# The fourth block of a recurrent layer's gates as three rounded products, gathered from the parts of the other blocks

## The chip, the cores and the metric

The kernel runs on one core of a Trainium2 chip. The metric is the device time of one execution in microseconds (us); before the change it is 1038.47 us, the median of 3 runs (1038.31 to 1038.69). Engines are named as in the profile: PE multiplies matrices, PEld is its weight load, DVE, ACT and POOL work on elements, and SP issues most transfers (its rows are marked SPq).

## The reference, cut to what matters

A two-layer decoder trunk takes one step on 1024 prompt tokens and 8 sequences of 4 sample tokens, 1056 columns in all. The first layer is a gated linear recurrence of width 1536, the second another recurrence that the change does not touch. In the first layer every token passes a projection, a short convolution that gives `xf`, and two gates whose weights are block diagonal, 16 blocks of 96 by 96:

```python
xh = xf.reshape(Bsz, T, N_BLK, BLK_W)                       # 16 blocks of 96
r  = sigmoid(einsum('btni,nij->btnj', xh, w_r).reshape(Bsz, T, W) + b_r)
ig = sigmoid(einsum('btni,nij->btnj', xh, w_i).reshape(Bsz, T, W) + b_i)
log_a = -LRU_C * softplus(-lam) * r
a = exp(log_a)
bterm = sqrt(-expm1(2.0 * log_a)) * (ig * xf)
_, h = associative_scan(_lru_combine, (a, bterm), axis=1)   # h[t] = a[t] h[t-1] + bterm[t]
```

## The kernel before, in words

Columns are cut into three chunks of 352 (`CH`). The layer's 1536 rows lie in 12 tiles of 128 rows; three tiles make a group `g` (0 to 3), and four blocks of 96 rows share a group. Tile `j` (0 to 2) holds block `j` and, in its rows 32j to 32j+31, a third of the fourth block. So blocks 0 to 2 are multiplied where they lie, and the fourth must first be gathered from three tiles.

Nearly all matrix work is done as three rounded products (`mm3`, lines 287 to 291): each operand is split into a rounded part and the rounded remainder, and high by high, high by low and low by high are summed in one accumulator. A convolution's result `t` is split that way into two slices of the tile `X` (`xpart`, lines 412 to 415; the split is on lines 596 and 597). The function `lru` (line 629) then computes the gates of a group, chunk by chunk, for both weights (`i` is 0 and 1): three rounded products for each of the three tiles (lines 653 and 654), a tanh into the tile `R`, and for the fourth block one product in full precision on 96 rows (line 659), a tanh into the tile `td`, and three transfers that put the thirds back into `R` (line 665). The fourth block's input comes from the tile `ST`: while a chunk is convolved, one transfer for each tile copies 32 rows of `t` there (line 594). Its weights `gs` are loaded as they are (line 639). After the gates follow exponentials, a square root, products and a scan on DVE, ACT and POOL.

The order of all this is not that of the code. Every operation is recorded with a rough cost, and with keys for what it reads and writes (`Flow`, line 61); a planner orders the operations of each engine by list scheduling, backward passes and a random search over the first part, and the program then has that order on every engine, each of which runs its own list from the top. A key names a tile or a piece of it: a write waits for the last reads of that key. Transfers from SP run through that one list too. Before the gates, each chunk of the input is normalised: squares are summed (ACT squares, line 491, DVE adds, line 493), PE sums over rows (line 326) and spreads the inverse root over the rows (line 545), and DVE scales eight tiles (line 550) and subtracts their rounded parts (line 374) to get what PE multiplies. With chunk 0 the scaling comes after the product instead. ACT also takes chunk 1's and 2's squares along rows of a transposed copy (line 532).

Of the kernel before, what the change touches and what calls it, by code (L numbers as in the profile page):

```python
# [14 lines left out]
F32 = mybir.dt.float32  # L15
F32R = mybir.dt.float32r
# [3 lines left out]
ALU = mybir.AluOpType  # L20
# [30 lines left out]
CH = 352  # L51
# [3 lines left out]
ML = WL // 128  # L55
# [202 lines left out]
def tile_trunk(ctx: ExitStack, tc: tile.TileContext, xT, xN, prm, hc, w0, wg, wo0, w1, wo1, s_in,  # L258
# [11 lines left out]
    def C(name, dt=F32):  # L270
        return work.tile([128, TOK], dt, tag="C", bufs=9, name=name)
# [12 lines left out]
    def chunk(c):  # L284
        return slice(c * CH, (c + 1) * CH)
# [59 lines left out]
    with ExitStack() as l0:  # L345
# [3 lines left out]
        def fixed(name, shape, dt=F32, pool=None):  # L349
            return (pool or pl).tile(shape, dt, tag=name, name=name)  # L350
# [7 lines left out]
        def dma(dst, src, r=(), w=(), prio=5, kb=180, q=Q, chain=None):  # L358
            fl.add("SP" if q is Q else "ACT", 0.45, lambda: q.dma_start(dst, src), r, w, prio, kb * (1.0 if r or fl.exact else 0.75),
                   line=chain)  # L360
# [8 lines left out]
        def pool(n, emit, r, w, prio=5):  # L369
            fl.add("POOL", 0.13 + 0.0022 * n if fl.exact else 0.1 + 0.00245 * n, emit, r, w, prio)  # L370
# [29 lines left out]
        hst = fixed("hst", [128, ML, 9])  # L400
# [153 lines left out]
        def conv(g, head=False):  # L554

            items = []
            for j in range(3):
                m = 3 * g + j
                mine = {}

                def evac(c, ps, pk, by=None, j=j, m=m, mine=mine):
                    n = CH if c < 2 else 1024 - 2 * CH
                    if c == 0:
                        mine[0] = next(xbs)
                        pool(3, lambda xb=mine[0][0]: G.memset(xb[:, :3], 0.0), (), (mine[0][1],), 2)
                    elif head:
                        mine[c] = next(xbs)
                        pool(3, lambda xb=mine[c][0]: G.tensor_copy(xb[:, :3], tails[:, 4 * j:4 * j + 3]), (("tail", j),), (mine[c][1],), 0)
                    xb, xk = mine[c]
                    t, tk = next(ts)  # L570
                    if by:
                        dve(n, lambda: V.tensor_tensor(xb[:, 3:3 + n], ps[:, :n], by[0], op=ALU.mult), (pk, by[1]), (xk,), 0)
                        pool(3, lambda: G.tensor_copy(tails[:, 4 * j:4 * j + 3], xb[:, n:n + 3]), (xk,), (("tail", j),), 1)
                    else:
                        act(n, lambda: S.copy(xb[:, 3:3 + n], ps[:, :n]), (pk,), (xk,), 0)
                    if c < 2 and not by:
                        nx, nk = mine[c + 1] = (tails[:, 4 * j:], ("tail", j)) if head else next(xbs)
                        act(3, lambda: S.copy(nx[:, :3], ps[:, CH - 3:CH]), (pk,), (nk,), 0)
                    parts = [(xb[:, :3 + n], t[:, :n], lambda ap, i: ap[:, i:i + n], n)]
                    if c == 2:  # L580
                        xs = xb[:, 323:379].rearrange("p (b j) -> p b j", j=7)
                        pool(24, lambda: G.tensor_copy(xs[:, :, :3], cs[:, m]), (("hct",),), (xk,), 1)
                        act(32, lambda: S.copy(xs[:, :, 3:], ps[:, n:CH].rearrange("p (b j) -> p b j", j=4)), (pk,), (xk,), 0)
                        pool(3, lambda: G.tensor_copy(cst[:, m, 0, :], xb[:, 320:323]), (xk,), (("cst", m),), 4)
                        pool(24, lambda: G.tensor_copy(cst[:, m, 1:, :], xs[:, :, 4:7]), (xk,), (("cst", m, 1),), 4)
                        parts.append((xs, t[:, n:].rearrange("p (b j) -> p b j", j=4), lambda ap, i: ap[:, :, i:i + 4], 32))
                    for src, dst, sh, u in parts:
                        act(u, lambda src=src, dst=dst, sh=sh: S.activation(dst, sh(src, 3), AF.Identity, bias=pc("cb", m),  # L588
                                                                         scale=pc("cw", 36 + m)), (xk, ("P",)), (tk,), 1, 0.1)
                        for k in range(3):  # L590
                            dve(u, lambda src=src, dst=dst, sh=sh, k=k: V.scalar_tensor_tensor(  # L591
                                dst, sh(src, k), pc("cw", 12 * k + m), dst, op0=ALU.mult, op1=ALU.add), (xk, tk), (tk,), 1, True)
# [36 lines left out]
        def lru(g):  # L629
            for i, n in ((0, 4), (4, 2)):  # L630
# [5 lines left out]
                act(u, lambda raw=raw, hi=hi, u=u: S.copy(hi, raw[:, :u]), (rk,), (("gh", i),), 2)  # L636
                pool(u, lambda raw=raw, hi=hi, lo=lo, u=u: G.tensor_tensor(lo, raw[:, :u], hi.bitcast(F32), op=ALU.subtract),
                     (rk, ("gh", i)), (("gl", i),), 2)
            dma(gs.rearrange("p a b -> p (a b)"), wg[g][:96, 768:], (), (("gs",),), 2, 74, chain=SPQ)
            prev = [(0.0, None)] * 3  # L640
            for c in range(NCH):
                s = c % 2
# [1 line left out]
                ab = a_rows[s].rearrange("p (j n) -> p j n", j=3)  # L644
                ta, ti = R[:, 0], R[:, 1]
                tak, tik = ([("R", s, i, j) for j in range(3)] for i in range(2))
                for i, hb in ((0, hbr), (1, hbi)):
                    for j in range(3):
                        m = 3 * g + j
                        ps, pk = next(hg)  # L650
                        (a, ak), (b, bk) = xpart(j, 0, c), xpart(j, 1, c)
                        u = 3 * i + j
                        fl.add("PE", 0.48, lambda ps=ps, a=a, b=b, u=u: mm3(ps[:, :CH], (gh[:, u, :], gl[:, u, :]), a, b, True, True),
                               (ak, bk, ("gh", u // 4 * 4), ("gl", u // 4 * 4)), (pk,), 0)
                        act(CH, lambda ps=ps, R=R, i=i, j=j, hb=hb, m=m: S.activation(R[:, i, j], ps[:, :CH], AF.Tanh, bias=hb[:, m:m + 1],  # L655
                                                                           scale=0.5), (pk, ("sm",)), (("R", s, i, j),), 2, 0.05)
                    ps, pk = next(hg)

                    fl.add("PE", 0.62, lambda ps=ps, i=i, c=c: T.matmul(ps[:96, :CH], gs[:, i, :], ST[:96, chunk(c)], start=True, stop=True),  # L659
                           (("gs",), *(("ST", j, c) for j in range(3))), (pk,), 0)  # L660
                    act(CH, lambda ps=ps, i=i: S.activation(td[:, i], ps[:96, :CH], AF.Tanh, bias=hbd[:96, 4 * i + g:4 * i + g + 1],
                                                            scale=0.5), (pk, ("sm",)), (("td", i),), 2, 0.05)
# [19 lines left out]
                for j in range(3):  # L682
# [13 lines left out]
                           (("a", s, j), tik[j], *((ppk,) if ppk else ())), (hk,), 3, both=True)  # L696
                    prev[j] = h[:, CH - 1:CH], hk
                    if c == 2:
                        pool(1, lambda h=h, m=m: G.tensor_copy(hst[:, m, 0:1], h[:, 319:320]), (hk,), (("hst", m),), 4)
                        pool(8, lambda h=h, m=m: G.tensor_copy(hst[:, m, 1:], h[:, 320:].rearrange("p (b j) -> p b j", j=4)[:, :, 3]),  # L700
                             (hk,), (("hst", m, 1),), 4)
                    if late:
                        continue
                    sg, sk = sgs[g][j, c]
# [356 lines left out]
        dma(h_out, hst.rearrange("p m b -> p (m b)"), [("hst", m) for m in range(ML)] + [("hst", m, 1) for m in range(ML)], (), 8)  # L1061
        out_last(x1b)
        for i, c in ((0, 0), (0, 1), (1, 0), (1, 1), (0, 2), (1, 2)):
            first1(i, c)
# [923 lines left out]
```

## Time and profile before

| what | value |
|---|---|
| runs of the kernel, median (lowest to highest) | 1038.47 us (1038.31 to 1038.69) |
| span of the profiled execution | 1036.8 us |
| what lies around the span, against the median | 1.7 us |
| PE busy | 1027.5 us (99%), 9789 matrix instructions |
| DVE, ACT, POOL busy | 794.4, 591.1, 500.0 us (77, 57, 48%) |
| share of PE in the chain that ended last | 95% |
| DVE busy from 60 to 160 us, and from 360 to 420 us | 94.20 of 100, 55.52 of 60 us |
| the full-precision product of the fourth block (L659) | 48 instructions, 458 ns each |

A row of the timeline has the start and the duration in us, the engine, the line of the code, the operation, the output and the inputs by the program's names, the shapes, how many were merged, and in brackets how long the engine stood idle before and what ended that. A product in full precision shows as two matrix instructions. A matrix instruction's duration runs over its successor's start, so what one costs PE is read from the distance between starts. The granted clock is 0.998 of full speed over the span.

### The profile page before, as it was taken

The page shows a single profiled execution, that of the slowest core. Times are in us where ns is not written, and L with a number is a line of the kernel's source. Part 1 is how long each engine was busy: PE and PEld are TensorE (multiplying, and loading weights), DVE is VectorE, ACT ScalarE, POOL GpSimd, SP SyncE. Part 2 cuts the span into 40 slices and gives each one's busy share as a digit, 9 for nine tenths or more (in the row PEclk, how much of TensorE's full clock was granted, in tenths as well). Part 3 has the DMA queues.
Part 4 walks back from the last instruction along what each step waited for, and adds up shares of the span by engine and source line. Part 5 has one row for each costly group of instructions (what it writes and reads, how often), then busy time and mean ns, then how long its engine had stood idle before and what let it go on. Part 6 is the DMA issues. An engine that isn't in the chain of part 4 may idle for free.

```text
span 1036.8 us, 25400 instructions
## 1 busy us (share of the span) xinstructions
PE 1027.5 (99%) x9789; PEld 998.9 (96%) x9789; DVE 794.4 (77%) x1548; ACT 591.1 (57%) x1346; POOL 500.0 (48%) x577
## 2 busy tenths in 40 slices
PE   9999999999999999999999999999999999999997
PEld 9999999999999999999999999999999999999986
DVE  5898996888897599355498986887869696985437
ACT  6678657867675775234355464737464555752324
POOL 2334553354443365644617565554645555541544
PEclk9999999999999999999999999999999999999999
DMA  8611112223751585444654241423233242658204
GB/s 280 196 37 49 53 50 75 61 62 112 231 166 55 174 275 184 145 154 153 196 173 145 76 158 41 152 71 126 83 107 122 84 143 86 211 159 252 87 1 168
DMA packets 92810, 133.56 MB, mean 129 GB/s; under 512 B 11728, under 2 KB 70096, under 8 KB 92688
## 3 DMA queue, kind: packets, MB, share of 16 engines
q1 hardware_dynamic: 84048, 117.14, 35.5%
q10 hardware_dynamic: 8640, 14.79, 4.5%
q8 instruction: 77, 1.26, 0.5%
q14 instruction: 45, 0.37, 0.1%
HBM read 88.81 MB, written 38.20 MB: 123 GB/s over the span
## 4 chain that ended last, share of the span: by engine, by line
PE 95%; DVE 2%; DMA 1%; ACT 1%; POOL 0%; issue 0%; ACTq 0%; POOLq 0%; DVEq 0%
PE mm L289 27%; PE mm L291 26%; PE mm L290 26%; PE hg L1202 2%; PE hg L659 1%; PE hg L289 1%; PE hg L291 1%; PE hg L290 1%; PE hg L1417 1%; PE hg L1419 1%; PE hg L1365 1%; PE mm L1365 1%; PE hg L1461 1%; DMA a<-in_w_dram 1%; DMA sg<-in_xT_dram 1%; PE hg L1287 0%
## 5 line engine op out<-in xcount | busy, mean ns | idle before, releaser
L289 PE MATMUL mm<-xh,whi 128*128 128x352 f32 (+1 forms) x1127 | 351.8, 312 | 0.0
L291 PE MATMUL mm<-xh,wlo 128*128 128x352 f32 (+1 forms) x1127 | 347.7, 309 | 0.0
L290 PE MATMUL mm<-xl,whi 128*128 128x352 f32 (+1 forms) x1127 | 347.2, 308 | 0.0
L374 POOL TENSOR_TENSOR wlo<-wraw,whi 128x256 fp32r<-128x256 f32 (+3 forms) x180 | 196.7, 1111 | 194.3 <-ACT whi L433 108.5
L290 PEld LDWEIGHTS mm<-xl,whi 128*128 128x128 f32 x1127 | 212.2, 188 | 1.7
L289 PEld LDWEIGHTS mm<-xh,whi 128*128 128x128 f32 x1127 | 211.9, 188 | 1.9
L291 PEld LDWEIGHTS mm<-xh,wlo 128*128 128x128 f32 x1127 | 211.8, 188 | 0.0
L591 DVE SCALAR_TENSOR_TENSOR k<-xb,prm_sb,k 128x352 f32<-128x352 f32 (+2 forms) x144 | 87.6, 616 | 12.7 <-ACT k L588 7.6
L289 PE MATMUL mm<-t,whi 128*128 128x264 f32 (+1 forms) x330 | 96.8, 293 | 0.0
L290 PE MATMUL mm<-t,whi 128*128 128x264 f32 (+1 forms) x330 | 94.4, 286 | 0.0
L291 PE MATMUL mm<-t,wlo 128*128 128x264 f32 (+1 forms) x330 | 94.4, 286 | 0.0
L374 POOL TENSOR_TENSOR wlo<-R,whi 128x256 fp32r<-128x256 f32 x78 | 67.2, 885 | 44.8 <-ACT whi L1582 33.1
L674 POOL TENSOR_TENSOR k<-X 128x352 f32<-128x352 f32 x36 | 43.4, 1216 | 58.1 <-DVE R L675 41.1
L1659 DVE TENSOR_TENSOR k<-mm,k 128x264 f32<-128x264 f32 x118 | 49.6, 425 | 24.1 <-PE mm L291 22.8
L289 PEld LDWEIGHTS mm<-t,whi 128*128 128x128 f32 x330 | 62.1, 188 | 1.3 <-DVE sg L1659 0.3
L291 PEld LDWEIGHTS mm<-t,wlo 128*128 128x128 f32 x330 | 62.2, 188 | 0.0
L290 PEld LDWEIGHTS mm<-t,whi 128*128 128x128 f32 x330 | 62.1, 188 | 0.0
L433 ACT CAST whi<-wraw 128x512 fp32r<-128x512 f32 (+2 forms) x79 | 44.1, 571 | 25.4 <-PE mm L290 9.3
L289 PE MATMUL mm<-yh,whi 128*128 128x352 f32 x153 | 50.0, 327 | 0.0
L291 PE MATMUL mm<-yh,wlo 128*128 128x352 f32 x153 | 49.4, 323 | 0.0
L290 PE MATMUL mm<-yl,whi 128*128 128x352 f32 x153 | 49.4, 323 | 0.0
L655 ACT ACTIVATE R<-hg,smalls 128x352 f32<-128x352 f32 x72 | 37.5, 553 | 17.9 <-DVE R L695 10.7
(482 smaller groups left out, 2502.7 us busy)
## 6 DMA issues: line engine op xcount, KB each, us to landing
wraw<-in_w_dram SPq DMA_DIRECT2D x54, 256.0 KB, 3.0
wraw<-in_w_dram ACTq DMA_DIRECT2D x34, 256.0 KB, 3.5
wraw<-in_wo_dram SPq DMA_DIRECT2D x34, 192.0 KB, 2.5
R<-in_w_dram ACTq DMA_DIRECT2D x19, 256.0 KB, 2.6
si<-in_s_in_dram SPq DMA_DIRECT2D x8, 512.0 KB, 5.9
vt<-sg SPq DMA_DIRECT2D x8, 512.0 KB, 3.1
sg<-vt SPq DMA_DIRECT2D x32, 128.0 KB, 3.0
kt<-kt SPq DMA_DIRECT2D x8, 512.0 KB, 2.6
```

The source lines that it names most:

```text
L289: T.matmul(out, wh, xh, start=first, stop=False, skip_group_check=more)
L290: T.matmul(out, wh, xl, start=False, stop=False, skip_group_check=more)
L291: T.matmul(out, wl, xh, start=False, stop=last, skip_group_check=more)
L374: emit = lambda: e.tensor_tensor(b, x, a.bitcast(F32), op=ALU.subtract)
L433: act(m, lambda: S.copy(hi[:, :m], raw[:, :m]), rk, (hk,), prio, chain=chains[0])
L591: dve(u, lambda src=src, dst=dst, sh=sh, k=k: V.scalar_tensor_tensor(dst, sh(src, k), pc("cw", 12 * k + m), dst, op0=ALU.mult, op1=ALU.add ...
L655: act(CH, lambda ps=ps, R=R, i=i, j=j, hb=hb, m=m: S.activation(R[:, i, j], ps[:, :CH], AF.Tanh, bias=hb[:, m:m + 1], scale=0.5), (pk, ("s ...
L659: fl.add("PE", 0.62, lambda ps=ps, i=i, c=c: T.matmul(ps[:96, :CH], gs[:, i, :], ST[:96, chunk(c)], start=True, stop=True), (("gs",), *((" ...
L674: pool(CH, lambda x=x, a=a, b=b: G.tensor_tensor(x, a.bitcast(F32), b.bitcast(F32), op=ALU.add), (ak, bk), (xk,), 3)
L1202: T.matmul(ps[32 * j:32 * j + 32, n * w:n * w + w], B[:, o:o + 32], q(slice(o, o + 32)), start=True, stop=True, tile_position=(0, 32 * j))
L1365: T.matmul(ps[:, n * 128:(n + 1) * 128], kt[:, 4 * i + n, :], vt[:, 4 * i + n], start=True, stop=True)
L1659: dve(QT, lambda: V.tensor_tensor(o[0], z[0], u[0], op=ALU.add), (z[1], u[1]), (o[1],), 0)
```

## The change

The fourth block is multiplied as three rounded products too. Its input is no longer copied from `t` to `ST`; instead, in `lru`, six transfers for each group and chunk gather 32 rows of each tile's high and low part from `X` into a new tile `fo` (one buffer for all chunks). Its weights are loaded into one of the three rotating buffers `wraw`, rounded on ACT into `gsh`, and the remainder goes by POOL into `gsl`. The freed tile `ST` takes over what `td` held (its first 704 columns) and the last states `hst` (the next 108), and keys say so.

```diff
-        td = fixed("td", [96, 2, CH])
+        fo = fixed("fo", [96, 2, CH], F32R)
+        gsl = fixed("gsl", [96, 2, 96], F32R)
...
-        gs = fixed("gs", [96, 2, 96])
+        gsh = fixed("gsh", [96, 2, 96], F32R)
...
+        td = ST[:96, :2 * CH].rearrange("p (i n) -> p i n", i=2)
+        hst = ST[:, 2 * CH:2 * CH + 9 * ML].rearrange("p (m b) -> p m b", m=ML)
...
-                    w = slice(32 * j, 32 * j + 32)
-                    dma(ST[w, chunk(c)], t[w], (tk,), (("ST", j, c),), 1, 45)
...
-            dma(gs.rearrange("p a b -> p (a b)"), wg[g][:96, 768:], (), (("gs",),), 2, 74, chain=SPQ)
+            raw, rk = next(raws)
+            his_, los_ = (o.rearrange("p a b -> p (a b)") for o in (gsh, gsl))
+            dma(raw[:96, :192], wg[g][:96, 768:], (), (rk,), 2, 74, chain=SPQ)
+            act(192, lambda raw=raw: S.copy(his_, raw[:96, :192]), (rk,), (("gs",),), 2)
+            pool(192, lambda raw=raw: G.tensor_tensor(los_, raw[:96, :192], his_.bitcast(F32), op=ALU.subtract),
+                 (rk, ("gs",)), (("gsl",),), 2)
...
+                for j in range(3):
+                    w = slice(32 * j, 32 * j + 32)
+                    for i in range(2):
+                        x, xk = xpart(j, i, c)
+                        dma(fo[w, i].bitcast(F32), x[w].bitcast(F32), (xk,), (("fo", i, j),), 1, 45)
...
-                    fl.add("PE", 0.62, lambda ps=ps, i=i, c=c: T.matmul(ps[:96, :CH], gs[:, i, :], ST[:96, chunk(c)], start=True, stop=True),
-                           (("gs",), *(("ST", j, c) for j in range(3))), (pk,), 0)
+                    fl.add("PE", 0.48, lambda ps=ps, i=i: mm3(ps[:96, :CH], (gsh[:, i, :], gsl[:, i, :]), fo[:, 0], fo[:, 1], True, True),
+                           (("gs",), ("gsl",), *(("fo", n, j) for n in range(2) for j in range(3))), (pk,), 0)
...
-                        dma(R[w, i, j], td[w, i], (("td", i),), (("R", s, i, j),), 2, 45)
+                        dma(R[w, i, j], td[w, i], (("ST", j, i),), (("R", s, i, j),), 2, 45)
```

Since the operations and their costs differ, the planner arrives at another order for the first part of the program. From the last gate product of the last group on, PE's list is the same, and so are the other engines' from about the first chunk of the first layer's last projection on.

The first place is SP's list at the start of the program, behind the first weights. `sg` and `k` from `in_xN` are transposed input for the squares by rows, `a`, `ST` and `wraw` are weights of the first projection, `xo` is a piece of the input that is used again much later. Before:

```order
L359 DMA sg<-in_xN_dram 128x1024
L359 DMA a<-in_w_dram 128x512
L359 DMA ST<-in_w_dram 128x512
L359 DMA k<-in_xN_dram 128x1024
L359 DMA wraw<-in_w_dram 128x512
L359 DMA xo_139<-in_xT_dram 128x352
L359 DMA wraw<-in_w_dram 128x512
```

And now:

```order
L359 DMA sg<-in_xN_dram 128x1024
L359 DMA xo_140<-in_xT_dram 128x352
L359 DMA a<-in_w_dram 128x512
L359 DMA ST<-in_w_dram 128x512
L359 DMA k<-in_xN_dram 128x1024
L359 DMA wraw<-in_w_dram 128x512 x2
```

The transfer of `xo` has moved ahead of four larger ones. The second place is ACT's list at the same time, where squares for the sum (line 491 before, 493 now), squares by rows (line 532, now 534) and roundings of weights stand. Before:

```order
L491 ACTIVATE xb_134<-sg 128x352
L491 ACTIVATE R<-sg 128x352 x3
L532 ACTIVATE sg,nr_133<-sg 128x1024
L433 CAST yh_152<-a 128x512
L433 CAST yh_152<-ST 128x512
L491 ACTIVATE R<-sg 128x352 x3
L491 ACTIVATE xo_138<-sg 128x352
```

And now:

```order
L493 ACTIVATE xb_135<-sg 128x352
L493 ACTIVATE R<-sg 128x352
L534 ACTIVATE sg,nr_134<-sg 128x1024
L493 ACTIVATE R<-sg 128x352 x2
L435 CAST yh_152<-a 128x512
L435 CAST yh_152<-ST 128x512
L493 ACTIVATE R<-sg 128x352 x3
L493 ACTIVATE xo_139<-sg 128x352
```

The square by rows now stands ahead of two squares that stood ahead of it. The third place is DVE's list around the third chunk's scaling (line 550, now 552). `k<-xb` are steps of the convolution, `smalls` short constants, `xl` the remainders that PE needs, `k<-ident` what PE spreads. Before:

```order
L540 TENSOR_TENSOR k<-ident,nr_132 128x256
L543 TENSOR_SCALAR k<-ident,nr_132 128x96
L833 TENSOR_TENSOR smalls<-smalls 128x12 x2
L833 TENSOR_SCALAR smalls<-smalls 128x12
L833 SCALAR_TENSOR_TENSOR smalls<-smalls 128x12 x8
L550 SCALAR_TENSOR_TENSOR R<-R,g_166,hg 128x352 x3
L374 TENSOR_TENSOR xl<-R,xh 128x352
```

And now:

```order
L624 SCALAR_TENSOR_TENSOR sg<-sg,mm 128x352
L593 SCALAR_TENSOR_TENSOR k<-xb_135,prm_sb,k 128x352 x2
L597 TENSOR_TENSOR X<-k,X 128x352 x3
L843 TENSOR_TENSOR smalls<-smalls 128x12 x2
L843 TENSOR_SCALAR smalls<-smalls 128x12
L843 SCALAR_TENSOR_TENSOR smalls<-smalls 128x12 x3
L593 SCALAR_TENSOR_TENSOR k<-xb_136,prm_sb,k 128x352
L843 SCALAR_TENSOR_TENSOR smalls<-smalls 128x12 x4
L552 SCALAR_TENSOR_TENSOR R<-R,g_166,hg 128x352 x8
L374 TENSOR_TENSOR xl<-R,xh 128x352
```

The eight scalings now stand together, behind convolution steps of the first chunk that stood later before. On PE the spread that they read has 33 rows between itself and the third chunk's first product, where it had 69; that product itself stands three rows earlier than before.

More of the change, by code (lines that the diff above doesn't have):

```diff
@@ L399, in tile_trunk @@
         cst = fixed("cst", [128, ML, 9, 3])
-        hst = fixed("hst", [128, ML, 9])
         tails = fixed("tails", [128, 12])
@@ L657, in lru @@
                     ps, pk = next(hg)
-                    fl.add("PE", 0.62, lambda ps=ps, i=i, c=c: T.matmul(ps[:96, :CH], gs[:, i, :], ST[:96, chunk(c)], start=True, stop=True),
-                           (("gs",), *(("ST", j, c) for j in range(3))), (pk,), 0)
+                    fl.add("PE", 0.48, lambda ps=ps, i=i: mm3(ps[:96, :CH], (gsh[:, i, :], gsl[:, i, :]), fo[:, 0], fo[:, 1], True, True),
+                           (("gs",), ("gsl",), *(("fo", n, j) for n in range(2) for j in range(3))), (pk,), 0)
                     act(CH, lambda ps=ps, i=i: S.activation(td[:, i], ps[:96, :CH], AF.Tanh, bias=hbd[:96, 4 * i + g:4 * i + g + 1],
-                                                            scale=0.5), (pk, ("sm",)), (("td", i),), 2, 0.05)
+                                                            scale=0.5), (pk, ("sm",)), [("ST", j, i) for j in range(3)], 2, 0.05)
                     for j in range(3):
                         w = slice(32 * j, 32 * j + 32)
-                        dma(R[w, i, j], td[w, i], (("td", i),), (("R", s, i, j),), 2, 45)
+                        dma(R[w, i, j], td[w, i], (("ST", j, i),), (("R", s, i, j),), 2, 45)
                 for j in range(3):
@@ L698, in lru @@
                     if c == 2:
-                        pool(1, lambda h=h, m=m: G.tensor_copy(hst[:, m, 0:1], h[:, 319:320]), (hk,), (("hst", m),), 4)
+                        pool(1, lambda h=h, m=m: G.tensor_copy(hst[:, m, 0:1], h[:, 319:320]), (hk,), (("ST", m, "h"),), 4)
                         pool(8, lambda h=h, m=m: G.tensor_copy(hst[:, m, 1:], h[:, 320:].rearrange("p (b j) -> p b j", j=4)[:, :, 3]),
-                             (hk,), (("hst", m, 1),), 4)
+                             (hk,), (("ST", m, "hs"),), 4)
                     if late:
@@ L1060, in tile_trunk @@
         dma(c_out, cst.rearrange("p m b j -> p (m b j)"), [("cst", m) for m in range(ML)] + [("cst", m, 1) for m in range(ML)], (), 8)
-        dma(h_out, hst.rearrange("p m b -> p (m b)"), [("hst", m) for m in range(ML)] + [("hst", m, 1) for m in range(ML)], (), 8)
+        dma(h_out, hst.rearrange("p m b -> p (m b)"), [("ST", m, o) for m in range(ML) for o in ("h", "hs")], [("ST", j, 2) for j in range(3)], 8)
         out_last(x1b)
```

## The prediction

> **What bounds the kernel now.** I read the page first: PE is busy for 1027.5 of 1036.8 us and holds 95% of the chain that ended last. Then who PE waited for (line, tile, waited-for engine, us in total, times, longest).
>
> ```profile
> PE 95%; DVE 2%; DMA 1%; ACT 1%; POOL 0%; issue 0%; ACTq 0%; POOLq 0%; DVEq 0%
> PE hg L821 <- DVE nr L501: 1.1, 1, 1.1
> PE hg L326 <- DVE xb L493: 0.8, 1, 0.8
> PE hg L326 <- ACT sg L1904: 0.4, 1, 0.4
> ```
>
> Three waits in a millisecond: one before the first instruction, one at 22 us for the sum of the first chunk's squares (L326), one in the last stage. Between 22 us and the second layer PE streams without a wait. So the time is PE's list, added up, and an edit is worth what it takes from that list, less each wait that it brings. Waits elsewhere cost nothing until PE's list has to stop.
>
> What the list's entries cost is read from the distance between starts. This is PE around the first fourth-block product.
>
> ```profile
> 65.93 0.32 PE L289 MATMUL hg<-X,gh 128*128 128x352 f32 x1
> 66.09 0.32 PE L290 MATMUL hg<-X,gh 128*128 128x352 f32 x1
> 66.25 0.32 PE L291 MATMUL hg<-X,gl 128*128 128x352 f32 x1
> 66.41 0.33 PE L289 MATMUL mm<-xh,whi 128*128 128x352 f32 x1
> 66.57 0.32 PE L290 MATMUL mm<-xl,whi 128*128 128x352 f32 x1
> 66.73 0.32 PE L291 MATMUL mm<-xh,wlo 128*128 128x352 f32 x1
> 66.89 0.76 PE L659 MATMUL hg<-ST,gs 96*96 96x352 f32 x2
> 67.21 0.59 PE L289 MATMUL mm<-xh,whi 128*128 128x352 f32 x1
> 67.64 0.32 PE L290 MATMUL mm<-xl,whi 128*128 128x352 f32 x1
> L659 PE MATMUL hg<-ST,gs x48: 457/458/461, 66.9 to 363.9; 96*96 96x352 f32 x48
> L545 PE MATMUL hg<-k,ones x6: 457/458/459, 26.6 to 47.3; 128*128 128x352 f32 x6
> ```
>
> A gate's three rounded products take 66.41 - 65.93 = 0.48 us. From the rounded product at 66.73 to the one at 67.64 is 0.91 us; without the fourth block that is two steps of 0.16, so the full-precision pair takes 0.59 us. The last two rows (least, median and most ns) show that all 48 instructions are alike, and that 96 rows and columns cost what 128 by 128 cost.
>
> **The change part by part.** *PE.* 24 products (4 groups, 3 chunks, 2 weights) go from 0.59 to 0.48 us each: 24 x 0.11 = 2.64 us less. That a rounded product on 96 rows costs what one on 128 costs isn't in the trace; the bounds are nothing gained (it costs 0.59 again) and 2.64 us. I take 2.64, since the two full-precision rows agree to a nanosecond over the same difference.
>
> On this the Trainium skill ("FP8 and Floating Point Precision", section TensorE Precision Notes) says that true FP32 takes four passes through the array. Going to three would by that rule take off a quarter of 0.59, some 3.5 us over 24 products. The rows decide: the four passes take 0.59 and three rounded products 0.48, not 0.44.
>
> *Weights.* Four times a 96x192 rounding on ACT and a remainder on POOL are new, and a load goes through `wraw`. The nearest rows are the other gate weights (min/median/max, the least is 128x256):
>
> ```profile
> L636 ACT CAST gh<-wraw x8: 399/507/624, 41.8 to 320.3; 128x512 fp32r<-128x512 f32 x4, 128x256 fp32r<-128x256 f32 x4
> L637 POOL TENSOR_TENSOR gl<-wraw,gh x8: 734/1134/1637, 42.5 to 320.8; 128x512 fp32r<-128x512 f32 x4, 128x256 fp32r<-128x256 f32 x4
> 60.00:160.00 100.00, 100.00 (x614) 98.55 (x614) 94.20 (x185) 70.54 (x144) 46.93 (x58) 1.00 0.18 54
> ```
>
> At most 4 x 0.40 on ACT and 4 x 0.73 on POOL. In the tightest stretch (busy us of PE, PEld, DVE, ACT, POOL) ACT has 29 and POOL 53 of 100 us free: nothing. If that cover were gone, a late weight would delay one gate product. The change adds no work to DVE, which has 6 us free there.
>
> *Transfers.* 36 copies into `ST` become 72 into `fo`.
>
> ```profile
> wraw<-in_w_dram SPq DMA_DIRECT2D x54, 256.0 KB, 3.0
> ST<-k SPq DMA_DIRECT2D x36, 44.0 KB, 1.9
> R<-td SPq DMA_DIRECT2D x72, 44.0 KB, 2.2
> L359 SPq DMA_DIRECT2D ST<-k x36: 507/512/592, 44.8 to 350.7; - x36
> SPq L359 <- POOL wlo L374: 73.2, 37, 8.8
> SPq L359 <- DVE k L591: 42.6, 16, 7.2
> ```
>
> One is issued in 0.51 us and lands 1.9 us later. `fo` has one buffer, so a chunk's six can start only when the chunk before it has been multiplied: 6 x 0.51 + 1.9 = 5.0 us. In PE's new list the nearest two chunks are the first two of group 0, with 48 rows of 0.16 = 7.7 us between the second product of one and the first of the next; at the other chunk changes it is 51 to 174 rows. So at least 2.7 us are spare. They are eaten if SP's list is held up in front of the six: it waited for POOL 37 times, 2.0 us each in the mean (the row on POOL's `wlo`), 8.8 at most. Since weight loads stood between such waits before, and PE never waited, I take nothing; the upper bound is under the rivals.
>
> The Trainium skill speaks against this edit ("DMA: Bandwidth & Descriptors", Rules for kernel authors): many small transfers should be joined, since under 64 KB one pays mostly overhead. The trace agrees as to the cost of one (1.9 us for 44 KB against 3.0 for 256 KB). By it the sum changes only if PE waits for these transfers, which is the slower rival.
>
> *The first chunk's sum.* PE's only early wait grows. What leads up to it:
>
> ```profile
> GB/s 280 196 37 49 53 50 75 61 62 112 231 166 55 174 275 184 145 154 153 196 173 145 76 158 41 152 71 126 83 107 122 84 143 86 211 159 252 87 1 168
> 13.64 0.62 ACT L433 CAST X<-a 128x512 fp32r<-128x512 f32 x1 [1.26 <-DMA a<-in_w_dram]
> 14.56 1.26 ACT L491 ACTIVATE R<-sg 128x352 f32<-128x352 f32 x3
> 15.73 1.05 ACT L532 ACTIVATE sg<-sg 128x1024 f32<-128x1024 f32 x1
> 18.97 0.48 ACT L491 ACTIVATE xo<-sg 128x352 f32<-128x352 f32 x1
> 18.72 1.59 POOL L374 TENSOR_TENSOR yl<-ST,yh 128x512 fp32r<-128x512 f32 x1
> 15.08 1.79 DVE L493 TENSOR_TENSOR xb<-xb,R 128x352 f32<-128x352 f32 x3
> 18.33 3.00 DVE L493 TENSOR_TENSOR xb<-xb,R 128x352 f32<-128x352 f32 x3 [1.46 <-ACT R L491]
> 21.43 0.52 DVE L493 TENSOR_TENSOR xb<-xb,xo 128x352 f32<-128x352 f32 x1
> ```
>
> The adds wait for ACT's squares (the 1.46 in brackets), and three of them take 3.00 us beside POOL's subtraction where three took 1.79 alone. Now ACT's square by rows stands two places earlier: it could start near 14.95 instead of 15.73. Its data are 0.5 MB right behind the weights that ACT had to wait for until 13.6; at the 280 GB/s of the first of 40 slices (first row) that is 1.87 us, so they land near 15.45. ACT would stand idle for 0.5 us, and all squares behind it, the rounding that POOL subtracts from, and the sum come 0.5 us later. Bounds: 0 (the data land sooner) and 1.15 us (the moved `xo`, 0.18 MB or 0.65 us, delays the two weights behind it as well). I take 0.5, as worked out.
>
> *The third chunk's start.* The spread now stands closer to its use. Before:
>
> ```profile
> 47.03 0.75 PE L545 MATMUL hg<-k,ones 128*128 128x352 f32 x2
> 48.60 1.56 DVE L550 SCALAR_TENSOR_TENSOR R<-R,g,hg 128x352 f32<-128x352 f32 x3
> 50.08 0.52 DVE L374 TENSOR_TENSOR xl<-R,xh 128x352 fp32r<-128x352 f32 x1
> 58.70 0.32 PE L289 MATMUL mm<-xh,X 128*128 128x352 f32 x1
> 39.28 0.53 DVE L621 SCALAR_TENSOR_TENSOR sg<-k,sg 128x352 f32<-128x352 f32 x1 [0.93 <-ACT k L620]
> 41.55 0.58 DVE L591 SCALAR_TENSOR_TENSOR k<-xb,prm_sb,k 128x352 f32<-128x352 f32 x1 [0.97 <-ACT k L588]
> ```
>
> The first remainder was there at 50.6, 8 us ahead of PE. Now 33 rows (5.3 us) lie between the spread's end and the first product, and the second rounded product needs the remainder another 0.16 later: 5.5 us. In them DVE makes all eight scalings (8 x 0.52 = 4.2) and the remainder (0.5): 4.7, and 0.2 for two hand-overs. So 0.6 us are spare, if DVE has come through the convolution steps ahead of the scalings in time; of the waits before it, two alone were 0.9 us. Bounds: 0 and the 1.9 us that these two waits would add. I take 0, the nearer, as the spare time covers one of them.
>
> *The rest of the order* up to 400 us differs in many places, and I take nothing for it: the cover is that PE's rows there wait for work done several us before, as the waits show of before. The last group's gates end some 9 us later in PE's list, but the product that needs them is 30 us behind; without that cover those 9 us would be paid.
>
> Sum: 1036.8 - 2.64 + 0.5 = 1034.66 us of span, and 1.67 us around it as now: 1036.3.
>
> **The rivals.** *All of the gain* (nothing lost at the sum): 1038.5 - 2.6 = 1035.8. For it speaks that the square's data may have landed; against it the order above. *The third chunk comes late*: with 0.5 and up to 1.9 us lost the gain is 0.2 to 1.6, around 1037.4. For it: DVE is the fullest engine beside PE; against it: PE never waited there in spite of that. *Slower, because PE waits for the gathers*: SP, held up by a weight load that waits for POOL, issues the six late. It decides from 2.7 us of hold-up on, at eight places (two chunk changes in each of four groups). With hold-ups like the mean of SP's waits for DVE's `k` added to POOL's (2.7 + 2.0 = 4.7) PE would wait 1.5 to 2.0 us; at half of the places that is 6.8 us: 1038.5 - 2.6 + 6.8 = 1042.7. Against it: two such hold-ups must meet, and before, the same queue with the same waits never made PE wait. *The change doesn't do what it says*: on 96 rows three rounded products cost 0.59 again, and the time stays at 1038.5 to 1038.9. Against it stand the two full-precision rows.
>
> **How the numbers follow.** A measurement of this kernel tells changes from about 0.2% on (2.1 us): faster is below 1036.4, slower above 1040.5. The forecast gets 0.42; its own range, 1035.9 to 1036.8, lies across the bound, and three quarters of it are faster (0.32). All of the gain 0.15, faster. The third chunk late 0.24, the same but for 0.01 slower. The gathers 0.11: 0.09 slower, 0.02 the same. No cheaper product 0.08, the same. Faster 0.47, the same 0.43, slower 0.10. The range for 8 in 10 leaves out the gathers' upper part and a little below the full gain: 1035.3 to 1038.9.
>
> **What would show it.** On PE, three rows `hg<-fo,gsh` and `gsl` with 0.16 us between starts instead of the pair (else the first term is wrong). The wait for the first chunk's sum: about 1.3 us where 0.8 stood; ACT idle before its first square by rows. At the third chunk's first product (near 58.7 us) no wait; a wait for DVE's `xl` there is the second rival. Between 60 and 400 us no wait of PE for `fo`; waits for transfers there mean the slower rival. The forecast is wrong if PE waits anywhere by more than 2 us in all that it didn't before.

## The result and the profile after

The changed kernel takes 1041.62 us in the median of 9 runs (1040.54 to 1047.02), the kernel before 1038.47 (1037.68 to 1038.99) on the same chip. The ratio is 1.0039, with a 95% interval of 1.003 to 1.0049: slower by 3 to 5 us where 2.2 less were forecast. The profiled execution has a span of 1039.8 us, 3.0 more than before. The runs of the changed kernel lie further apart than those before (one took 1047.02 us, the other eight 1040.54 to 1042.68); why was not looked into.

The chain that ended last gave PE 95% before, DVE 2 and DMA 1. Of the changed kernel:

```profile
PE 88%; DVE 5%; DMA 3%; ACT 2%; issue 1%; SPq 1%; POOL 0%; ACTq 0%; POOLq 0%; DVEq 0%
```

And the waits of PE (line, tile, waited-for engine, us in total, times, longest), three lines before, eight now:

```profile
PE mm L289 <- DVE k L736: 1.3, 1, 1.3
PE hg L831 <- DVE nr L503: 1.1, 1, 1.1
PE hg L289 <- DMA fo<-X: 0.6, 1, 0.6
PE hg L289 <- ACT ST L671: 0.5, 1, 0.5
PE hg L326 <- ACT sg L1914: 0.4, 1, 0.4
PE hg L289 <- ACT R L665: 0.3, 1, 0.3
PE hg L290 <- DMA fo<-X: 0.3, 1, 0.3
PE mm L289 <- DVE sg L619: 0.2, 1, 0.2
```

Five of the six new lines lie between 263 and 378 us, in the groups 2 and 3; the last one, on L619, is at 33 us. There the gates share PE's list with `out` (lines 727 to 738), which adds each product to a residual that SP has to load first. I summed by how much PE's starts lie further apart than is usual for the same pair of instructions: from 250 to 300 us it is 3.31 us (0.08 before), from 350 to 400 us 1.60 (0 before). With the 2.64 us that the product was to save this gives +2.2 of the +3.0 us of span; the other 0.8 is spread too thin to place. Little of it comes from the start: the 361st matrix instruction, ahead of the first product of a fourth block, starts at 60.73 us now and at 60.64 before. At 400 us the two kernels stand 3.1 us apart, and at the end they still do.

The new waits one by one, on PE (timeline: start, duration, instruction, in brackets the wait and what ended it):

```profile
263.54 0.32 PE L289 MATMUL hg<-fo,gsh 96*96 96x352 f32 x1
...
263.86 0.32 PE L291 MATMUL hg<-fo,gsl 96*96 96x352 f32 x1
265.48 0.43 PE L289 MATMUL mm<-yh,whi 128*128 128x352 f32 x1 [1.30 <-DVE k L736]
...
275.26 0.37 PE L289 MATMUL hg<-fo,gsh 96*96 96x352 f32 x1 [0.63 <-DMA fo<-X]
```

The third rounded product starts 0.32 us after the first, so they stand 0.16 apart, as forecast. Right behind them stands the largest new wait: a product of `out` has no free bank (one of the accumulators that products are summed in), because DVE has not yet added the residual to an older one. Why DVE was late stands on DVE and SP:

```profile
254.80 3.68 SPq L359 DMA_DIRECT2D fo<-X  x6
258.58 0.53 SPq L359 DMA_DIRECT2D x1a<-xo  x1
259.20 0.52 SPq L359 DMA_DIRECT2D R<-ST  x1
259.78 0.58 SPq L359 DMA_DIRECT2D xo<-in_xT_dram  x1
260.45 0.38 SPq L359 DMA_DIRECT2D x1a<-k  x1
260.92 0.38 SPq L359 DMA_DIRECT2D k<-in_xT_dram  x1
...
264.90 0.53 DVE L736 TENSOR_TENSOR k<-mm,k 128x352 f32<-128x352 f32 x1 [4.55 <-DMA k<-in_xT_dram]
```

SP issues almost without a pause, and the six gathers take 3.68 us of its list in one piece. That they stand together has a likely reason in the one buffer of `fo`: the product of the chunk before frees it for all six at once. A second buffer was not tried. SP doesn't come to them at that moment: PE started that product's last instruction at 251.69 us, 3.1 us before the first gather. The write-back of a gate (`R<-ST`) and the residual (`k<-in_xT`) stand behind them. Before, the same stretch read

```profile
260.05 0.41 SPq L359 DMA_DIRECT2D k<-in_xT_dram  x1
260.56 1.78 SPq L359 DMA_DIRECT2D R<-td  x3
...
263.91 0.52 DVE L726 TENSOR_TENSOR k<-mm,k 128x352 f32<-128x352 f32 x1 [2.67 <-DMA k<-in_xT_dram]
```

DVE already waited 2.67 us for a residual then, and PE did not notice. At 4.55 it does. (The adds stand in another order, so the two waits need not be for the same load; the pairs shown further down are.) Of the other new waits, 0.9 us in two rows are for `fo` itself, and two are for ACT's tanh, behind late write-backs: between 345 and 385 us DVE waited 9.4 us for `R<-ST` where it waited 0.5 for `R<-td` before, and ACT 6.3 where it waited 4.5.

### The profile page after: what moved, and what is told of

Its sections match the earlier page's. It is cut to its first block, busy times and chain, and to the rows that moved or that the text cites. A ratio compares the mean times of both kernels' runs of the same rounds, so it can differ in the third digit from the quotient of the medians.

```text
span 1039.8 us, 25483 instructions
## 1 busy us (share of the span) xinstructions
PE 1028.6 (99%) x9813; PEld 1001.8 (96%) x9813; DVE 791.6 (76%) x1548; ACT 594.5 (57%) x1350; POOL 503.6 (48%) x581
## 4 chain that ended last, share of the span: by engine, by line
PE 88%; DVE 5%; DMA 3%; ACT 2%; issue 1%; SPq 1%; POOL 0%; ACTq 0%; POOLq 0%; DVEq 0%
PE mm L289 25%; PE mm L291 24%; PE mm L290 24%; PE hg L1212 2%; PE hg L1427 1%; DVE k L593 1%; PE hg L289 1%; PE hg L291 1%; PE hg L290 1%; PE hg L1429 1%; DMA R<-in_xN_dram 1%; PE hg L1375 1%; PE mm L1375 1%; DMA R<-ST 1%; PE hg L1471 1%
## 5 line engine op out<-in xcount | busy, mean ns | idle before, releaser
L685 DVE SCALAR_TENSOR_TENSOR R<-R,k 128x352 f32<-128x352 f32 x36 | 25.5, 719 | 27.9 <-DMA R<-ST 24.4
```

Of the source, the lines that this page charges most:

```text
L685: dve(CH, lambda x=x, j=j, ti=ti: V.scalar_tensor_tensor(ti[:, j], ti[:, j], 1.0, x, op0=ALU.add, op1=ALU.mult), (xk, tik[j]), (tik[j],), ...
```

## The experiments

Theory A: the extra issues on SP delay what stands behind them in SP's list, in groups 2 and 3. Rival B: the planner's other order is worse by itself. Rival C: the lone buffer makes the gathers come late for PE. Rival D: the rounded product itself brings the loss. Later, A2: it is not the number of issues but their place. All ratios are to the kernel before on the same chip, with 95% intervals.

### The product alone

```diff
-  T.matmul(ps[:96, :CH], gs[:, i, :], ST[:96, chunk(c)], start=True, stop=True)
+  mm3(ps[:96, :CH], (gh[:96, 3*i, :96], gl[:96, 3*i, :96]), xpart(0, 0, c)[0][:96], xpart(0, 1, c)[0][:96], True, True)
```

> The kernel before with every engine's order as it was; only the fourth block's product is issued as three rounded products (on 96 rows of block 0's parts and weights, which are there already; the 36 copies into ST go on, unused). What it leaves out: the fourth block's own input and weights. If the term of the product is right (24 x 0.11 us): 1035.8, ratio 0.9975, and no new wait. Rival D (the rounded product itself brings the loss, since PE runs ahead of the engines that feed it in groups 2 and 3): 1038 or more, with new waits of PE there.

Measured: 1036.2 us, ratio 0.998 (0.9971 to 0.999); span 1034.5. PE's rows at the first triple on 96 rows, its first instruction and the one behind its third:

```profile
66.59 0.32 PE L289 MATMUL hg<-X,gh 96*96 96x352 f32 x1
...
67.06 0.32 PE L289 MATMUL mm<-xh,whi 128*128 128x352 f32 x1
```

0.47 us for the triple. The starts of the same products in both traces draw apart by 1.97 us over the 18 triples up to 268 us, 0.11 each. At 274 us 0.6 us are given back, since PE, now 2.3 us earlier, waits for a bank of `out`. So the gain is real and rival D falls, but for those 0.6 us. (By 34 us, ahead of any such product, this execution is 0.3 us in front; so 2.0 of the 2.3 us of span are the product's, 2.6 less 0.6.) At the residual of 264 us DVE waits 3.28 us here, and PE still does not notice:

```profile
262.46 0.53 DVE L726 TENSOR_TENSOR k<-mm,k 128x352 f32<-128x352 f32 x1 [3.28 <-DMA k<-in_xT_dram]
```

### The same order, joined gathers

A tile's high and low part lie side by side in `X`, so one transfer can fetch both. Here it stands at the place of the second of the two, and nothing at the first; no other operation moves.

```diff
-  dma(fo[w, i].bitcast(F32), x[w].bitcast(F32), (xk,), (("fo", i, j),), 1, 45)
+  b = (6 * c + 2 * j) * CH        # emitted for i == 1 only
+  dma(fo[w].rearrange("p i n -> p (i n)").bitcast(F32), X[w, b:b + 2 * CH].bitcast(F32), (xk,), (("fo", i, j),), 1, 45)
```

> The change with its own order on every engine, but one gather of a tile's high and low part at the place of the second of its two, and nothing at the first: 36 issues fewer on SP, no operation moved. Theory A (the number of issues on SP, order apart): most of the 5 us of waits in groups 2 and 3 go, 1036 to 1037.5, ratio 0.998. Rival B (the order itself is worse, the transfers cost nothing): 1041 to 1042 as the change.

Measured: 1037.24 us, ratio 0.9993 (0.9983 to 1.0002); span 1035.9, 3.9 less than the change. The place that cost most, again:

```profile
254.48 1.78 SPq L359 DMA_DIRECT2D fo<-X  x3
...
258.71 0.38 SPq L359 DMA_DIRECT2D k<-in_xT_dram  x1
...
262.29 0.53 DVE L738 TENSOR_TENSOR k<-mm,k 128x352 f32<-128x352 f32 x1 [2.26 <-DMA k<-in_xT_dram]
```

The block is 1.9 us shorter, the residual is issued 2.2 us earlier (0.3 of it this execution was ahead already), DVE waits 2.26 instead of 4.55 us, and PE does not wait here. Of the distances over the usual, 0.66 us is left between 250 and 300 us and nothing from 350 on. DVE's wait for `R<-ST` between 345 and 385 us falls from 9.4 to 2.3 us. Since the order is the change's own, rival B falls in its plain form. Of rival C 0.9 us is left: the buffer is still the only one, and no wait for `fo` is in the list of this version. Between 250 and 285 us SP issues 58 transfers in 29.6 us here and 58 in 29.4 in the change, but that is because it is further down its list: the same stretch of it, from a weight load at 250 us to `x1a<-xb` at 285, takes 34.4 us in the change and 30.8 here. Joining makes the issues fewer and the pieces shorter at once, so this run does not tell which of the two counts.

### Another seed, with and without the change

The planner's random search starts from another seed (`Random(2)` for `Random(1)`).

> The change as it is, with another seed of the random search that orders the first 60 us; the work and the transfers are the same. Theory A: the same overfilled SP in groups 2 and 3, 1040 to 1043 us. Rival B (an unlucky order): the time moves by more than 2 us, to 1038 or below.

> The kernel before with another seed of the random search, the work unchanged. Rival B (orders differ by some us anyway): off 1038.4 by 2 us or more, to either side. Theory A: within 1 us of 1038.4, since SP has the same 36 copies, spread out.

Measured: the change from the other seed 1042.06 us, ratio 1.0037 (1.0024 to 1.005); the kernel before from the other seed 1038.47, ratio 1.0002 (0.9993 to 1.0011). In both pairs the time stays, but this says nothing on the orders in groups 2 and 3. The search works on the first part of the program, and the traces show how little came of it further down: from 240 to 400 us every engine of the change has the same list with either seed, and the kernel before has the same list up to 400 us on every engine. Other orders of groups 2 and 3 come with the planner's other price, below.

### Twice as many issues, in two places

From the kernel with the product alone, in the order of before. First, every copy into `ST` at the convolutions is issued twice:

```diff
   dma(ST[w, chunk(c)], t[w], (tk,), (("ST", j, c),), 1, 45)
+  Q.dma_start(ST[96:, chunk(c)], t[w])        # in the same operation
```

> As the product alone in the order of before, and each of the 36 copies into ST is issued twice, the second time into 32 unused rows of ST: 36 issues more on SP, spread over the convolutions, order otherwise as before. Theory A in its plain form (any 36 issues more overfill SP): 1039 to 1041, with waits of PE in groups 2 and 3. If it is the block of six in a row at the gates that does it, and not the number: about 1036, as the product alone.

Measured: 1038.05 us (1035.87 to 1040.05), ratio 0.9995 (0.9984 to 1.0005); span of the profiled execution 1034.1, with a wait of 1.2 us at 274 us, where the product alone had one of 0.3. The median speaks for a loss of 1.5 us against the product alone, with intervals that overlap. The profiled execution, the fastest of the ten, speaks for 1.2: it was 0.9 us further ahead by 34 us, when no copy had been doubled yet, and 0.4 behind by 400. So 36 more issues at the convolutions cost 0 to 3 us, most likely a little over one. The same number at the gates:

```diff
   dma(R[w, i, j], td[w, i], (("td", i),), (("R", s, i, j),), 2, 45)
+  Q.dma_start(ST[96:, chunk(c)], td[w, 0])    # in the same operation, i == 0 only
```

> As the product alone in the order of before (block 0's parts in place of the fourth block's), and each of the 36 transfers that put the first weight's gate back from td into R is issued twice, the second time into unused rows of ST: 36 issues more on SP, this time at the gates, 18 of them in groups 2 and 3 among out()'s loads. Theory A2 (not the number of issues but that they stand in the two stretches where SP already issues without a pause): 1038 to 1040, new waits of PE between 250 and 290 and between 345 and 385 us of 2 us or more in all. If issues at the gates are as harmless as those at the convolutions: 1036 to 1036.5 and under 1 us of such waits.

Measured: 1048.24 us, ratio 1.0104 (1.0089 to 1.0119). This is more than the expectation allowed, and the experiment was not clean: the three second copies of a chunk go to the same rows, each waits until the one before has landed, and SP stands still meanwhile (from 240 to 400 us):

```profile
SPq L667 <- DMA ST<-td: 8.8, 9, 2.7
```

So it was made again with three different destinations (`ST[96:, chunk(j)]`).

> As the doubled issues at the gates (product alone in the order of before, block 0's parts in place of the fourth block's), but the three second copies of a chunk go to three different places in ST, so that none of them waits for the one before to land, as they did there (nine such waits of 1 us between 240 and 400 us). What is left is the issue time alone: 36 more on SP, 9 of them in each of groups 2 and 3. Theory A2 (issue time in front of out()'s loads): 3 x 0.6 = 1.8 us more in front of the loads at each of six chunk changes; 1037 to 1040, with 1 to 4 us of new waits of PE in groups 2 and 3. If issue time alone is harmless and only a queue that stands still costs: 1036 to 1036.5.

Measured: 1042.32 us, ratio 1.0038 (1.0025 to 1.0052): 0.58% or 6 us more than the product alone, from 36 issues and 1.6 MB. SP's list and DVE, then the new waits of PE:

```profile
256.55 0.54 SPq L359 DMA_DIRECT2D R<-td  x1
257.14 0.58 SPq L667 DMA_DIRECT2D ST<-td  x1
257.78 0.58 SPq L359 DMA_DIRECT2D R<-td  x1
...
259.67 0.59 SPq L667 DMA_DIRECT2D ST<-td  x1
...
263.34 0.38 SPq L359 DMA_DIRECT2D k<-in_xT_dram  x1
...
266.18 0.53 DVE L728 TENSOR_TENSOR k<-mm,k 128x352 f32<-128x352 f32 x1 [6.38 <-DMA k<-in_xT_dram]
```

```profile
PE mm L289 <- DVE k L728: 1.9, 2, 1.1
PE mm L289 <- DVE xb L728: 1.3, 1, 1.3
PE mm L289 <- DVE xo L728: 1.2, 1, 1.2
PE mm L291 <- POOL wlo L375: 1.0, 1, 1.0
```

It is the picture of the change again, made from the order of before: a piece of 3.7 us ahead of the residual, DVE waiting 6.38 us for it instead of 3.28, PE without a bank. (The last row stands at 394 us; ahead of it ACT had waited 3.26 us for a write-back.) A2 stands: the same 36 issues cost some 6 us at the gates and 0 to 3 at the convolutions. The upper end of its forecast (1040) was too low, though PE paid less than the issues take: 18 of the 36 stand in groups 2 and 3, at 0.59 us each 10.6 us, of which PE lost about 6.

### The planner told what an issue costs

The planner prices every issue at 0.45 us. Transfers of 32 rows take 0.51 us alone and 0.61 in a row of six (3.68 / 6).

```diff
-  fl.add("SP" if q is Q else "ACT", 0.45, ...
+  fl.add("SP" if q is Q else "ACT", 0.6 if kb in (45, 90) else 0.45, ...
```

> The change with one number of the planner's model changed: an issue of a transfer of 32 rows costs 0.6 us of SP instead of 0.45, as the trace shows it. If the loss comes from a plan that did not know what its issues cost: the waits in groups 2 and 3 shrink by half or more, 1037 to 1039. If SP is simply full there, no plan helps: 1040 to 1043.

> The kernel before, planned anew with 0.6 us for each transfer of 32 rows, nothing else. If the gain of the joined gathers with that number (2.2 us) is the better plan's and not the product's: about 1036 here too. If the product brings it and the plan only takes the waits away: 1038 to 1038.6, the same as before, since before had no waits in groups 2 and 3 to take away.

Measured: the change, so planned, 1038.48 us (1036.13 to 1041.76), ratio 1.0005 (0.9995 to 1.0016): by the median the loss is gone, the gain is not there. The time came as expected, the mechanism only in part: 1.80 us of distances over the usual are left from 250 to 300 and 1.68 from 350 to 400, 3.5 of 4.9, so the waits did not shrink by half. The profiled execution (span 1037.4) is 2.4 us shorter than that of the change, and 0.7 of that was there by 34 us. The six gathers still stand in one piece at 252 us (3.69 us), with the write-backs and residuals placed otherwise around them. The kernel before, so planned: 1038.01, ratio 0.9999 (0.999 to 1.0008), as the second expectation has it: there was no wait to take away. So rival B is right in another form: the same work has orders that differ by some 3 us here. That the planner missed the better one because its price was too low is likely, but only one plan with the new price was run.

### Joined, and planned anew

> The change with one gather for a tile's high and low part together (they lie side by side in X): 36 transfers of 90 KB instead of 72 of 45 KB, nothing else. Theory A (number of issues on SP): the six-issue blocks of 3.7 us become blocks of about 1.8 us, most of the 5 us of waits in groups 2 and 3 go: 1036 to 1037.5 us, ratio 0.998. Theory C (the lone buffer: a chunk's gathers can only start after the product of the chunk before): shorter chain, so better too, but PE's waits for the fo transfers stay above 0.5 us. Rival B (order): no systematic effect, 1038 to 1042.

> One gather for a tile's high and low part, planned anew with 0.6 us for each transfer of 32 rows. Theory A2: waits in groups 2 and 3 below 0.7 us, as with the joined gathers in the change's own order; what the start of the program adds depends on the order found: 1036 to 1038.

> Joined gathers, planned with 0.6 us for each transfer of 32 rows, and another seed of the random search. If the version is better for its fewer issues and its planner's number, and not for one lucky order: 1035.5 to 1037, ratio 0.997 to 0.999. If it was a lucky order: 1038 or more.

Measured: planned with 0.45 us, 1038.04, ratio 0.9998 (0.9989 to 1.0007). Planned with 0.6, 1036.07, ratio 0.998 (0.997 to 0.9989); one of its ten runs took 2559 us, as no other run of any kernel did, and is not in the ratio. With another seed 1036.22, ratio 0.9981 (0.9972 to 0.9989). The last two beat the kernel before by some 2 us, and not by one lucky order: here the seed did change the lists between 240 and 400 us. PE's waits of the version with 0.6 us, all of them:

```profile
PE hg L831 <- DVE nr L503: 1.1, 1, 1.1
PE hg L326 <- ACT sg L1914: 0.5, 1, 0.5
PE mm L289 <- issue: 0.4, 1, 0.4
PE mm L290 <- DVE xl L978: 0.2, 1, 0.2
```

None is in groups 2 and 3. The version planned with 0.45 us lost its gain elsewhere, by the profiled execution, which is the slowest of its ten (1039.79):

```profile
PE mm L290 <- DVE xl L374: 1.2, 1, 1.2
PE mm L289 <- DVE xb L736: 1.1, 1, 1.1
```

The first is at 58 us, at the third chunk's second product, the second at 379 us for a late residual.

### Three that missed

The gathers of the change from ACT's queue:

> The change with the 72 gathers issued from ACT's queue instead of SP's. Theory A: SP's list is 36 issues shorter than before the change, residual loads and write-backs of R are on time, and ACT, busy 57 percent, takes about 0.5 us for each issue: 1036 to 1038 us. Theory C (the lone buffer and its chain of six issues): the same six issues in a row remain, so PE waits for fo as now, about 1.3 us, and 1040 or more. If ACT is overfilled instead: PE waits for ACT's tanh, 1040 or more with waits on ACT.

Measured: 1041.43 us, ratio 1.003 (1.0017 to 1.0043). SP had more room (29.0 us of issues between 345 and 385 us, 33.9 in the change), but PE's waits only changed hands (on ACT's tanh into `ST` 1.6 us, on DVE's residual adds 1.5). The six of a chunk stand together here too, and ACT computes nothing while it issues them (its queue, then the row behind it):

```profile
364.90 5.81 ACTq L359 DMA_DIRECT2D fo<-X  x6
370.81 1.28 ACT L671 ACT_TABLE_LOAD   x1 [5.32 <-DMA fo<-X]
```

On this the Trainium skill ("DMA: Bandwidth & Descriptors", section Issuing engines are not separate DMA queues) says that issuing from several engines saves only the time of issuing, which is usually small beside the transfer. Here that time is not small: one gather holds its engine for 0.51 to 0.61 us and lands after 1.9, and 36 issues more at the gates cost 6 us above.

The transfers as before, the high and low part made on chip:

```diff
+  act(CH, lambda: S.copy(fo[:, 0], ST[:96, chunk(c)]), ...)
+  pool(CH, lambda: G.tensor_tensor(fo[:, 1], ST[:96, chunk(c)], fo[:, 0].bitcast(F32), op=ALU.subtract), ...)
```

> The rounded product kept, the transfers as before: one copy of 32 rows of t for each tile and chunk goes into ST (36 in all), and the high and low part of the gathered 96 rows are made there, by one rounding on ACT and one subtraction on POOL for each chunk. What it leaves out: the first chunk's second gate of the fourth block is held rounded. Theory A (SP's list is overfilled in groups 2 and 3 by the 36 extra issues, and transfers behind them come late): no waits of PE in groups 2 and 3 above 0.5 us in all, the product's 2.6 us stay, so about 1036 us, ratio 0.997 to 0.999. Rival B (the planner's other order, whatever the transfers): anything from 1036 to 1042. Rival D (the rounded product itself costs PE more than its starts show): 1040 or more.

Measured: 1045.83 us, ratio 1.0077 (1.0062 to 1.0092). This was meant as the product alone and was not: the rounding waits in ACT's list for PE's last read of the lone buffer, and write-backs are late as well. Two of ACT's waits, the first from 250 to 285 us, the second from 345 to 385:

```profile
ACT fo L654 <- PE hg L291: 2.7, 1, 2.7
...
ACT a L680 <- DMA R<-ST: 7.9, 2, 4.3
```

It shows that this version loses more than the change; which part of it costs how much stays open.

Both gathers and write-backs joined (one transfer for both gates of a tile, after the second gate):

> One gather for a tile's high and low part, and one transfer that puts both gates' thirds back into R (3 in place of 6 for a chunk, after the second gate): 72 transfers in all at the gates, where before it were 108 and in the change 144. Theory A2: no waits in groups 2 and 3 from SP; the first gate reaches R some 2 us later, which PE notices only if the banks fill up. 1035.8 to 1037, ratio 0.998.

Measured: 1039.38 us, ratio 1.0012 (1.0002 to 1.0022). The fewest issues of all, and a miss: at 259 us PE waits 1.0 us for ACT's tanh, which itself stood 1.65 us for POOL (the last copy out of its target in `R`). That copy waited for DVE's scan. Whether the later first gate made the scan late was not shown.

## Why the prediction was wrong

*What bounds the kernel* was right as far as it went: PE's list, added up. But from "PE streams without a wait" I took it that the engines that feed PE had much to spare. How much, DVE's waits tell: 2.67 us for a residual at 264 us before, 3.28 with the product alone, both unnoticed by PE; 4.55 in the change's order is noticed, and so is 6.38 in the order of before.

*PE* (24 x 0.11 = 2.64 us) was right. A triple on 96 rows takes 0.47 to 0.48 us, and each of 18 saved 0.11; alone, the edit took 2.3 us off the span and 1.0 to 3.0 off the time.

*Weights* at nothing was right: no wait of PE names the new rounding, and none `gsh` or `gsl`.

*Transfers* at nothing is the step that failed. I asked only whether the six come in time for PE (5.0 us against 7.7) and what might stand in front of them. They were late, but PE waited only 0.9 us for them in all. Six took 3.68 us to issue and not 6 x 0.51 = 3.06, and at the four chunk changes in groups 2 and 3 SP came to them 2.8 to 6.6 us after the buffer was free, beyond the 2.7 that were spare. In front of them stood other issues, one behind the other, and not the waits for POOL that I had thought of. What I did not ask is what stands behind them in SP's list: 3.68 us in one piece ahead of residuals and write-backs, at chunk changes where SP has no pause. Price by the runs: the joined gathers in the same order take 3.9 us off the span; 36 issues put into the order of before at a like place cost 6 us. I had worked out what six issues cost, and used it only for the six. The page's rule that I set beside this edit (the Trainium skill, "DMA: Bandwidth & Descriptors", section Rules for kernel authors: join small transfers) pointed the right way: a joined one of 88 KB is issued in the time of one of 44 KB. I gave it weight only by way of PE waiting for `fo`.

*The first chunk's sum* (+0.5 us) was wrong in sign. The moved square did not stop ACT (it starts at 13.98 us without a wait, so its data had landed by then, where 15.45 was worked out), and PE's pause before the sum's product fell from 0.96 to 0.16 us:

```profile
13.98 1.06 ACT L534 ACTIVATE sg<-sg 128x1024 f32<-128x1024 f32 x1
...
20.77 0.32 PE L291 MATMUL mm<-xh,yl 128*128 128x352 f32 x1
21.10 0.78 PE L326 MATMUL hg<-ones,xb 128*128 128x1 f32 x6
```

Nor does the pause belong to the order alone: with the product alone, in the order of before, it is absent from the trace. And by 34 us both kernels are level (0.03 us apart), so it was worth nothing.

*The third chunk's start* at nothing was right, and nearly to the row:

```profile
53.52 4.02 DVE L552 SCALAR_TENSOR_TENSOR R<-R,g,hg 128x352 f32<-128x352 f32 x8
57.46 0.52 DVE L374 TENSOR_TENSOR xl<-R,xh 128x352 fp32r<-128x352 f32 x1
58.31 0.32 PE L289 MATMUL mm<-xh,X 128*128 128x352 f32 x1
```

The remainder is there at 57.98 and wanted at 58.47: 0.5 us to spare, where 0.6 was worked out. How thin that is the joined version planned with 0.45 us shows, which waited 1.2 us just there, in another order.

*The rest of the order* at nothing failed with the transfers. "Work done several us before", as I put it, held for the order before; in the new one that cover is eaten in groups 2 and 3. With the corrected price in the planner 3 us come back, by the median.

The rival *slower, because PE waits for the gathers* gave 1042.7, near the 1041.6 that came. Its number was nearly right by luck: of its mechanism (the six come late for PE) 0.9 us showed, most of the rest is what the six make late. The sign that was to show the forecast wrong, more than 2 us of new waits of PE, is what the trace has.

## What to carry to other kernels

A transfer on an in-order queue costs twice: when it lands, and by how long it holds back what stands behind it. Ask of each added issue which load follows it, who waits for that load, and how many microseconds that engine already waits for it without the bound engine noticing; those are the spare time. A change that makes the bound engine faster uses some of it up. When several issues stand in one piece, join them by layout, and give the planner the issue time that the trace shows.

## What the runs showed of the hardware

The time to issue a transfer does not go by its bytes. Of the changed kernel (least, median and most ns, first and last start):

```profile
L359 SPq DMA_DIRECT2D fo<-X x72: 507/542/1819, 45.6 to 368.9; - x72
L359 SPq DMA_DIRECT2D wraw<-in_wo_dram x58: 327/333/2148, 231.0 to 983.3; - x58
```

And of the version with joined gathers in the same order:

```profile
L359 SPq DMA_DIRECT2D fo<-X x36: 507/513/592, 49.9 to 361.2; - x36
```

44 KB in 32 rows take longer to issue than weights of mostly 192 and 256 KB in 128 rows, and twice the bytes in 32 rows take the same. Whether it is the number of rows that does it, their form, or that the gathers go from tile to tile while the weights come from DRAM, was not tried.
